# Folding the query norm's weights into the key norm's weights in a hybrid retention and sparse-attention layer

## The chip, the cores and the metric

The kernel runs on one core of one Trainium2 chip. The metric is the device time of one execution in microseconds, taken from runs of the whole program; a time of this kernel is the median of its runs. The engines are called as in the profile: PE (matrix products), PEld (its weight loads), DVE (vector), ACT (scalar, activations), POOL (GpSimd) and SP (the queue that issues the transfers).

## What is computed

One decoder layer on 1024 tokens with 16 meta tokens ahead of them. A normed stream is projected by one matrix; the columns feed a retention with 4 heads and a sparse attention with 8 heads of 64 columns, in which an indexer picks 256 keys for each query. Both results are projected, and a squared-ReLU MLP follows. What matters here is the norm of the attention's queries and keys:

```python
def rmsnorm(x, w):
    xf = x.astype(jnp.float32)
    y = xf * lax.rsqrt(jnp.mean(xf * xf, axis=-1, keepdims=True) + EPS)
    return y * w.astype(jnp.float32)

def sparse_attention(q, k, v, iq, ik, iw, q_gain, k_gain, rel_bias, pos, topk):
    qn = rmsnorm(q, q_gain) * (dh ** -0.5)       # q: (B,T,8,64)
    kn = rmsnorm(k, k_gain)                      # k: (B,T,64), one key for all heads
    ...
    logits = jnp.einsum('bchd,bckd->bchk', qb, k_sel)
```

Queries and keys meet only in that product over the 64 columns, and each of the two weight vectors has one entry for each column.

## The kernel before

The tokens are worked on in 8 blocks of 128. The code runs, in the order in which it is written, through these stages:

- The norm and the transposes of the input, block by block (`do_norm1`), the small projection (`small_proj`, the keys `kn` among it), the indexer's query projection (`index_q`, L246 to L248 into `psA`, copied to `nat`) and the indexer's scores (`index`): L356 and L357 on PE into `psB`, L359 on ACT into `rl`, L363 (L361 for the first head) on DVE, which adds up `sc`.
- The weights of the norms are loaded (`kgain` at L410, `qgain` at L412). The keys are normed (L432, DVE) and later transposed (L306).
- The query projection, L518 on: for each block the projection into `psA` (L246 to L248), a copy on ACT to `qn` (L528), its squares (L529, ACT), their sum (L531, DVE), the reciprocal root on POOL (L141, L142), the product with it (L533, DVE), the product with `qgain` (L534, POOL), and the store of the block to DRAM in `qd` (L535, SP). `qn` has the tag `rl` with two buffers, which it shares with `nat`; `psA` has three buffers, which index, query and retention projections share.
- The retention, for each of 4 heads: the weights are loaded (L210) and split into a high and a low half (L189 on ACT, L194 on POOL), then the meta tokens' part (`ret_meta`, L232 to L235) and 8 blocks (`ret_in`, L246 to L248 again, and `ret_out`). The split weights lie in 9 buffers of each half, which the weights of index, query and retention share, raw weights in 3.
- The search for the 256 keys by bisection (`topk`: L746 on DVE, L751 on ACT), the attention, the output projection and the MLP (L1002 to L1004, L1120 to L1122).

What stands on an engine's queue is not the order of the code. A planner that goes by a model of times puts every instruction into the queues and may move later work ahead; each queue then runs strictly in its order. So L432, which is written behind the indexer's last block, runs at 116 to 120 us, while the indexer's instructions go on to 197 us, and the bisection's L746, written near the end, runs from about 100 us on.

Of the kernel before, what the change touches and what calls it, by code (L numbers as in the profile page):

```python
# [14 lines left out]
ALU = mybir.AluOpType  # L15
# [66 lines left out]
def layer(ctx, tc, x, meta, norm1_w, w_in, ret_w, q_w, k_w, rel, w_out, norm2_w, w1, w2,  # L82
          ident_d, pack_d, hot_d, out, gam):
    nc = tc.nc
# [13 lines left out]
    def psA():  # L98
        return pp.tile([128, 512], F32, tag="A", name="psA", bufs=3)
# [18 lines left out]
    def bcast(src, n):  # L118
        return bass.AP(tensor=src.tensor, offset=src.offset, ap=[[0, 128], [1, n]])

    def shift(pool, n):

        nc.gpsimd.memset(pool.tile([128, n // 4], F32, name="shift", bufs=1), 0.0)
# [15 lines left out]
    def rsqrt(ms, k, f=1.0, P=128):  # L139
        y = small.tile([128, k], F32, name="rs_y", tag=f"rsy{k}", bufs=1 if k == 9 else 4)  # L140
        nc.gpsimd.tensor_tensor(y[:P], ms, epst[f][:P, :k] if isinstance(f, float) else f, op=ALU.add)  # L141
        nc.gpsimd.tensor_tensor(y[:P], y[:P], nhalf[:P, :k], op=ALU.pow)  # L142
        return y
# [97 lines left out]
    def proj(ps, b, hs, ls, c0, n):  # L241
        P = 128
        for d in range(8):
            uh, ul = u_sl(b, d)
            wh, wl = hs[d][:, c0:c0 + n], ls[d][:, c0:c0 + n]
            nc.tensor.matmul(ps[:P, :n], uh, wh, start=d == 0, stop=False)  # L246
            nc.tensor.matmul(ps[:P, :n], ul, wh, start=False, stop=False)  # L247
            nc.tensor.matmul(ps[:P, :n], uh, wl, start=False, stop=d == 7)  # L248
# [138 lines left out]
    for b in range(NB):  # L387
# [7 lines left out]
        if b:  # L395
# [13 lines left out]
    kgain = big.tile([128, 64], F32, name="kgain")  # L409
    nc.sync.dma_start(kgain, bcast(k_w, 64))  # L410
    qgain = big.tile([128, 64], F32, name="qgain")
    nc.sync.dma_start(qgain, bcast(q_w, 64))  # L412
    shift(const, 320)
    rgain = const.tile([128, 4], F32, name="rgain")
    nc.sync.dma_start(rgain, bass.AP(tensor=ret_w.tensor, offset=ret_w.offset, ap=[[1, 128], [128, 4]]))
# [12 lines left out]
                            op=ALU.add)  # L428
# [93 lines left out]
    for b in range(NB):  # L522
        ps = psA()
        proj(ps, b, hs, ls, 0, 512)
        p3 = ps.rearrange("p (h c) -> p h c", h=8)
        sq = big.tile([128, 8, 64], F32, tag="fg", name="sq", bufs=2)
        qn = wp.tile([128, 8, 64], F32, tag="rl", name="qn", bufs=2)
        nc.scalar.activation(qn, p3, AF.Copy)  # L528
        nc.scalar.activation(sq, qn, AF.Square)  # L529
        ssq = small.tile([128, 8], F32, name="ssq")  # L530
        nc.vector.tensor_reduce(ssq, sq, axis=mybir.AxisListType.X, op=ALU.add)  # L531
        r = rsqrt(ssq, 8, 64.0)
        nc.vector.tensor_tensor(qn, qn, r[:, :, None].to_broadcast([128, 8, 64]), op=ALU.mult)  # L533
        nc.gpsimd.tensor_tensor(qn, qn, qgain[:, None, :].to_broadcast([128, 8, 64]), op=ALU.mult)  # L534
        nc.sync.dma_start(qd[:, b], qn.rearrange("p a b -> p (a b)"))  # L535


# [655 lines left out]
def build(nc, inputs):  # L1193
    arrays, args = {}, []

    def add(name, a):
        arrays[name] = a
        args.append(nc.dram_tensor(name, a.shape, mybir.dt.from_np(a.dtype), kind="ExternalInput").ap())
    for name in _INS:
        a = np.ascontiguousarray(inputs[name])  # L1200
        if name in ("x", "w_in", "w_out", "w_ff1", "w_ff2"):
            a = a[0]
        add(f"in_{name}_dram", a)
    ident, pack, hot, gam = shape_constants()
    add("ident_dram", ident)
    add("pack_dram", pack)
    add("hot_dram", hot)
    args.append(nc.dram_tensor("out_0_dram", (T, D), F32, kind="ExternalOutput").ap())
    with tile.TileContext(nc, schedule_with_timeline_sim=True) as tc:
        layer(tc, *args, gam)  # L1210
    return arrays
# [10 lines left out]
```

## Time and profile before

| | |
|---|---|
| median of 3 runs | 1310.89 us (1308.47 to 1311.84) |
| the profiled execution's own time | 1311.07 us |
| its span | 1309.2 us |
| PE busy | 1248.5 us, 95% |
| DVE busy | 1037.7 us, 79% |
| ACT busy | 761.3 us, 58% |
| POOL busy | 236.2 us, 18% |
| granted TensorE clock, mean | 0.983 |

The span is the profiled part of an execution; 1.9 us of its own time lie around it. The granted clock is a share of the higher of TensorE's two levels (2.4 GHz): 1.00 in a stretch says that all of it ran at that level, 0.50 that all of it ran at 1.2 GHz. A busy share is an average over stages with different limits, so each stage is read by itself.

### The profile page before, as it was taken

Reading aid. Unit: us, or ns where it says so; the run is one execution under the profiler, and the core shown is the slowest. Engines: PE = TensorE matmul, PEld = TensorE weight load, DVE = VectorE, ACT = ScalarE, POOL = GpSimd, SP = SyncE. Lnnn points to the kernel's source line nnn. Section 1 sums busy time; section 2 is a strip of 40 time slices with the busy share of each in tenths; the row PEclk is TensorE's granted clock in tenths of the full one; section 3 lists DMA queues with packets and bytes.
Section 4 is the critical chain, followed back from the end, with each engine's and each line's share of the span. In section 5 each row is a group of like instructions: output and inputs, shape, how many; then the busy total and the mean of one; then the engine's idle time right before and its main releaser. Section 6 shows DMA issues by size and latency. Waiting matters only on the chain.

```text
span 1309.2 us, 18365 instructions
## 1 busy us (share of the span) xinstructions
PE 1248.5 (95%) x6032; PEld 1031.6 (79%) x6032; DVE 1037.7 (79%) x2297; ACT 761.3 (58%) x1612; POOL 236.2 (18%) x286
## 2 busy tenths in 40 slices
PE   5999989999999899999997999999999999999998
PEld 4888867777887677877786888888888888888887
DVE  5579999995459889976579887777788887887875
ACT  6567556787975777764356565555455444444442
POOL 4002373425244332200233000000000100000000
PEclk8999989999999899999998999999999999999999
DMA  8103031202021322212963444434539834344222
GB/s 277 61 18 91 17 97 63 74 9 73 9 73 39 131 98 83 84 60 89 324 225 119 169 145 153 145 145 144 186 129 345 327 112 181 137 153 173 94 95 97
DMA packets 101278, 165.05 MB, mean 126 GB/s; under 512 B 8712, under 2 KB 48944, under 8 KB 97472
## 3 DMA queue, kind: packets, MB, share of 16 engines
q1 hardware_dynamic: 101184, 163.90, 36.3%
q8 instruction: 47, 0.77, 0.2%
q14 instruction: 47, 0.39, 0.1%
HBM read 113.46 MB, written 51.85 MB: 126 GB/s over the span
## 4 chain that ended last, share of the span: by engine, by line
PE 69%; DVE 18%; ACT 5%; issue 3%; DMA 2%; POOL 1%; SPq 0%; ACTq 0%; DVEq 0%; POOLq 0%
PE psB L1121 5%; PE psB L1120 5%; PE psB L1122 5%; PE psB L1002 4%; PE psB L1003 4%; PE psB L1004 4%; PE psA L1003 4%; PE psA L1002 4%; PE psA L1004 4%; PE psA L246 3%; PE psA L247 3%; PE psA L248 3%; PE psA L1121 3%; PE psA L1120 3%; PE psA L1122 3%
## 5 line engine op out<-in xcount | busy, mean ns | idle before, releaser
L973 ACT ACTIVATE wh<-ga 128x512 fp32r<-128x512 f32 x144 | 87.5, 628 | 164.0 <-PE psB L1121 143.1
L246 PE MATMUL psA<-wh,uh 128*128 128x512 f32 x376 | 152.4, 406 | 2.9 <-DVE fg L487 2.2
L247 PE MATMUL psA<-wh,ul 128*128 128x512 f32 x376 | 150.1, 399 | 0.0
L248 PE MATMUL psA<-wl,uh 128*128 128x512 f32 x376 | 149.8, 399 | 0.0
L974 DVE TENSOR_TENSOR wl<-ga,wh 128x512 fp32r<-128x512 f32 x144 | 96.7, 688 | 49.4 <-ACT wh L973 48.8
L973 ACT ACTIVATE wh<-sum 128x512 fp32r<-128x512 f32 x128 | 78.8, 625 | 71.6 <-DVE sum L970 61.0
L751 ACT ACTIVATE jk_top<-sc,tcand 128x784 bf16<-128x784 f32 (+2 forms) x93 | 98.3, 1057 | 24.4 <-DVE tcand L821 20.3
L1121 PE MATMUL psB<-wh,wl 128*128 128x512 f32 x280 | 108.9, 389 | 0.0
L1122 PE MATMUL psB<-wl,wh 128*128 128x512 f32 x280 | 108.9, 389 | 0.0
L1120 PE MATMUL psB<-wh 128*128 128x512 f32 x280 | 106.8, 389 | 0.0
L974 DVE TENSOR_TENSOR wl<-sum,wh 128x512 fp32r<-128x512 f32 x128 | 88.6, 693 | 4.7 <-ACT wh L973 4.7
L246 PEld LDWEIGHTS psA<-wh,uh 128*128 128x128 f32 x376 | 71.9, 191 | 16.9 <-DVE fg L487 1.9
L248 PEld LDWEIGHTS psA<-wl,uh 128*128 128x128 f32 x376 | 71.7, 191 | 14.0
L247 PEld LDWEIGHTS psA<-wh,ul 128*128 128x128 f32 x376 | 71.8, 191 | 12.5
L1040 POOL COPY ga<-wl 128x1 f32<-128x1 f32 x8 | 6.6, 827 | 400.3 <-PE psB L1003 276.3
L746 DVE TENSOR_SCALAR_CACHE_REDUCE jk_cnt<-sc,tcand 128x400 bf16<-128x400 f32 (+2 forms) x93 | 70.3, 756 | 1.0
L359 ACT ACTIVATE rl<-psB,absw 128x320 f32<-128x320 f32 (+5 forms) x104 | 53.1, 556 | 31.0 <-DVE sc L363 16.8
L1121 PE MATMUL psA<-wh,wl 128*128 128x512 f32 x168 | 65.4, 389 | 0.0
L1122 PE MATMUL psA<-wl,wh 128*128 128x512 f32 x168 | 65.4, 389 | 0.0
L1120 PE MATMUL psA<-wh 128*128 128x512 f32 x168 | 64.9, 389 | 0.0
L194 POOL TENSOR_TENSOR wl<-wr,wh 128x512 fp32r<-128x512 f32 x44 | 61.3, 1419 | 19.0 <-ACT wh L189 15.6
L363 DVE SCALAR_TENSOR_TENSOR sc<-rl,sgnw,sc 128x320 f32<-128x320 f32 (+5 forms) x91 | 56.1, 651 | 8.2 <-ACT rl L359 7.2
(391 smaller groups left out, 3582.0 us busy)
## 6 DMA issues: line engine op xcount, KB each, us to landing
ga<-hid SPq DMA_DIRECT2D x28, 1024.0 KB, 5.2
wr<-in_w_ff_dram SPq DMA_DIRECT2D x34, 512.0 KB, 4.9
hid<-hs SPq DMA_DIRECT2D x48, 256.0 KB, 2.0
wr<-in_w_in_dram SPq DMA_DIRECT2D x32, 256.0 KB, 3.1
ysd<-ys SPq DMA_DIRECT2D x32, 256.0 KB, 2.4
ys<-ysd SPq DMA_DIRECT2D x32, 256.0 KB, 5.0
gb<-in_w_ff_dram SPq DMA_DIRECT2D x8, 1024.0 KB, 5.3
ga<-in_w_ff_dram SPq DMA_DIRECT2D x8, 1024.0 KB, 5.0
```

The costliest lines, as they stand in the source:

```text
L246: nc.tensor.matmul(ps[:P, :n], uh, wh, start=d == 0, stop=False)
L247: nc.tensor.matmul(ps[:P, :n], ul, wh, start=False, stop=False)
L248: nc.tensor.matmul(ps[:P, :n], uh, wl, start=False, stop=d == 7)
L751: nc.scalar.activation(jk_top[:, :ncol[i]], sc[i], AF.Sign, scale=-1.0, bias=cand[:, j:j + 1], accum_out=cnt[:, j:j + 1])
L973: nc.scalar.activation(view(hi), s, AF.Copy)
L974: nc.vector.tensor_tensor(view(lo), s, view(hi).bitcast(F32), op=SUB)
L1002: nc.tensor.matmul(ps, hi[:, a], uh[:, d], start=d == 0, stop=False)
L1003: nc.tensor.matmul(ps, lo[:, a], uh[:, d], start=False, stop=False)
L1004: nc.tensor.matmul(ps, hi[:, a], ul[:, d], start=False, stop=d == 3)
L1120: nc.tensor.matmul(ps[tb], ah[:, t], bh, start=j == 0 and m not in CONT, stop=False, skip_group_check=True)
L1121: nc.tensor.matmul(ps[tb], al[:, t], bh, start=False, stop=False, skip_group_check=True)
L1122: nc.tensor.matmul(ps[tb], ah[:, t], bl, start=False, stop=j == NO - 1, skip_group_check=True)
```

## The change

The two weight vectors are multiplied once, in place, right behind their loads, on DVE: `kgain` holds the product from then on, and the keys are normed with it. The multiplication of each query block with `qgain` on POOL is left out, and the store of the block follows the product on DVE.

```diff
     nc.sync.dma_start(kgain, bcast(k_w, 64))
     qgain = big.tile([128, 64], F32, name="qgain")
     nc.sync.dma_start(qgain, bcast(q_w, 64))
+    nc.vector.tensor_tensor(kgain, kgain, qgain, op=ALU.mult)
     shift(const, 320)
...
         nc.vector.tensor_tensor(qn, qn, r[:, :, None].to_broadcast([128, 8, 64]), op=ALU.mult)
-        nc.gpsimd.tensor_tensor(qn, qn, qgain[:, None, :].to_broadcast([128, 8, 64]), op=ALU.mult)
         nc.sync.dma_start(qd[:, b], qn.rearrange("p a b -> p (a b)"))
```

## Rows read from the trace of the kernel before

**Rows 1.** The page: span, busy time by engine, shares of the chain that ended last.

```profile
span 1309.2 us, 18365 instructions
PE 1248.5 (95%) x6032; PEld 1031.6 (79%) x6032; DVE 1037.7 (79%) x2297; ACT 761.3 (58%) x1612; POOL 236.2 (18%) x286
...
PE 69%; DVE 18%; ACT 5%; issue 3%; DMA 2%; POOL 1%; SPq 0%; ACTq 0%; DVEq 0%; POOLq 0%
```

**Rows 2.** Busy time by stretch: PE, PEld, DVE, ACT, POOL; granted clock; DMA share, GB/s.

```profile
140.00:174.00 34.00, 33.50 (x160) 28.43 (x159) 33.76 (x78) 20.94 (x41) 15.42 (x15) 1.00 0.08 32
174.00:190.00 16.00, 12.21 (x42) 8.33 (x41) 15.95 (x21) 8.00 (x17) 13.63 (x11) 0.68 0.54 153
...
720.00:1309.00 589.00, 585.29 (x2583) 484.30 (x2581) 468.27 (x749) 280.91 (x498) 8.26 (x18) 1.00 0.45 163
```

**Rows 3.** Timeline of PE: start, us, instruction [idle before it <- its releaser].

```profile
177.28 0.29 PE L232 MATMUL psA<-wl,um 128*16 128x256 f32 x1 [0.97 <-POOL wl L194]
...
185.59 0.63 PE L246 MATMUL psA<-wh,uh 128*128 128x512 f32 x1
```

**Rows 4.** Waits of PE, 60 to 206 us: in total, times, longest.

```profile
PE psA L246 <- ACT qn L528: 0.5, 1, 0.5
```

**Rows 5.** Timeline of POOL, 174 to 188 us.

```profile
174.25 2.97 POOL L194 TENSOR_TENSOR wl<-wr,wh 128x512 fp32r<-128x512 f32 x2
177.19 1.60 POOL L534 TENSOR_TENSOR qn<-qn,qgain 128x512 f32<-128x512 f32 x1
178.74 3.00 POOL L194 TENSOR_TENSOR wl<-wr,wh 128x512 fp32r<-128x512 f32 x2
181.71 1.59 POOL L534 TENSOR_TENSOR qn<-qn,qgain 128x512 f32<-128x512 f32 x1
183.27 4.23 POOL L194 TENSOR_TENSOR wl<-wr,wh 128x512 fp32r<-128x512 f32 x3
```

**Rows 6.** Timeline of DVE around the same stretch.

```profile
172.11 0.68 DVE L533 TENSOR_TENSOR qn<-qn,rs_y 128x512 f32<-128x512 f32 x1
172.71 1.00 DVE L363 SCALAR_TENSOR_TENSOR sc<-rl,sgnw,sc 128x320 f32<-128x320 f32 x2
...
174.32 1.78 DVE L533 TENSOR_TENSOR qn<-qn,rs_y 128x512 f32<-128x512 f32 x1
...
176.70 2.43 DVE L363 SCALAR_TENSOR_TENSOR sc<-rl,sgnw,sc 128x400 f32<-128x400 f32 x2
...
183.58 1.23 DVE L824 TENSOR_SCALAR tt<-tcnt 128x3 int32<-128x3 f32 x1
...
194.40 0.15 DVE L824 TENSOR_SCALAR tt<-tcnt 128x3 int32<-128x3 f32 x1
```

**Rows 7.** Timeline of ACT: two of the eight copies into `qn`.

```profile
166.25 0.60 ACT L528 ACTIVATE qn<-psA 128x512 f32<-128x512 f32 x1 [3.52 <-DMA qd<-qn]
...
184.17 0.59 ACT L528 ACTIVATE qn<-psA 128x512 f32<-128x512 f32 x1
```

**Rows 8.** Timeline of SP: the fifth store of a query block.

```profile
178.81 0.34 SPq L535 DMA_DIRECT2D qd<-qn  x1
```

**Rows 9.** Tile `qn`: duration ns min/median/max, first and last start us, forms.

```profile
L533 DVE TENSOR_TENSOR qn<-qn,rs_y x8: 680/686/1782, 137.9 to 199.3; 128x512 f32<-128x512 f32 x8
L534 POOL TENSOR_TENSOR qn<-qn,qgain x8: 1286/1295/1743, 138.8 to 200.4; 128x512 f32<-128x512 f32 x8
...
DMA to landing us min/median/max: 2.0/2.0/3.4
```

**Rows 10.** Tiles `kgain` and `qgain`, as rows 9.

```profile
L432 DVE SCALAR_TENSOR_TENSOR kn<-kn,rs_y,kgain x9: 269/273/1394, 116.0 to 120.3; 128x64 f32<-128x64 f32 x8, 16x64 f32<-16x64 f32 x1
...
L412 SPq DMA_DIRECT2D qgain<-in_q_norm_w_dram x1: 458/458/458, 11.7 to 11.7; - x1
...
DMA to landing us min/median/max: 3.2/3.2/3.2
```

**Rows 11.** Timeline of DVE in the start-up.

```profile
11.45 1.47 DVE L328 TENSOR_TENSOR wsl<-wrs,wsh 128x200 fp32r<-128x200 f32 x2
```

## The prediction, made before the changed kernel was run

> **What bounds the kernel now.** I read the page first [rows 1]. PE is busy 95% of the span and carries 69% of the chain that ended last, so in most of the kernel only what leaves PE without work, or lowers its clock, costs time. DVE carries another 18%, so the second question is where DVE takes PE's place. The busy times by stretch answer it [rows 2]. From 720 us on PE works 585.29 of 589.00 us: the MLP has nothing to give, and the change doesn't touch it. The lines that the change touches run from 138.8 to 202 us [rows 9]. From 140 to 174 us PE and DVE are both full (33.50 and 33.76 of 34.00 us). Then comes a hole: from 174 to 190 us PE works 12.21 of 16.00 us at a granted clock of 0.68, while DVE (15.95) is full and POOL (13.63) nearly so. The hole costs 16.00 - 12.21 = 3.8 us of idle PE and, as 0.68 of the clock means that 32% of the time's columns were not done, 0.32 x 16.00 = 5.1 us of lower clock: 8.9 us. Of TensorE's two levels 0.68 is 64% of the stretch at the lower one; the projection that starts at 185.59 us still takes 0.63 us for one matrix product there [rows 3]. The clock fell behind the idle pieces, at about 180 us.
>
> Who makes the hole? The waits of PE and the timelines of POOL, DVE, ACT and SP show two threads, and both run over POOL, whose queue has no gap from 174.25 to 187.50 us [rows 5].
> - Weights. The seven L194 there split the first retention head's weights. PE's L232 at 177.28 waited for one of them for 0.97 us [rows 3].
> - Buffers. The retention's first block projection, at 185.59, waited for a `psA` buffer until ACT's copy into `qn` of block 6, at 184.17 [rows 3, 4, 7]. Such a copy waits for the store of the block two before (block 4's own copy sat 3.52 us for one) [rows 7]. Block 4's product on DVE was done at 172.11 + 0.68 = 172.8 us [rows 6], but its L534 came up on POOL only at 177.19, behind other work, and its store left at 178.81 [rows 5, 8].
>
> A third effect is on DVE. While POOL works there, DVE's products stretch: a pair of L363 took 2.43 us against 1.00 for a somewhat smaller pair before, L533 1.78 against 0.68, a 128x3 `tt` 1.23 against 0.15 [rows 6].
>
> **The change part by part.** *Removed: eight L534 on POOL*, 1.3 us each, 1.6 in the hole [rows 5, 9]. Six of them lie outside the hole. There PE is full (140 to 174 us: 98.5%), so POOL's 6 x 1.3 us and what DVE gets back is covered by PE's own queue, and I cost it at nothing. If that cover were gone, each would return at most its own length to DVE, 6 x 1.3 = 7.8 us, and at least nothing, since DVE's counts and its reads of PSUM went on unstretched beside some of them.
>
> In the hole two go, 1.60 + 1.59 = 3.2 us of a POOL queue without gaps. The L194 behind them move up by as much, so the weights are ready up to 3.2 us sooner; and for 3.2 us DVE is not held. Both PE (through L194) and the last block of the indexer (through L363 on DVE) follow: -3.2 us. What is late next in that thread is the L194 themselves, some 10 us of which stay.
>
> *Moved: the stores.* The store's wait goes from POOL to DVE. Block 4's leaves SP's queue at about 172.8 and not at 178.81, 6.0 us sooner; block 5's at 174.32 + 1.78 = 176.1 and not behind the L534 that ends at 183.3, 7.2 us sooner [rows 5, 6, 8]. With 2.0 us to landing [rows 9], the buffer for block 6's copy is free at 174.8, and the copy at 184.17 could come up to 9 us earlier. SP has no other work between that is harmed: each store is still one issue, eight in all, and what is queued behind them (the next weights) moves up too. So the `psA` buffer stops being the retention's gate; the weights are. It can start with its first quarter of weights at about 177 us and then go at the pace of POOL's remaining L194.
>
> *The clock.* The trace of before doesn't show what the clock does when the hole narrows. Nothing returns if PE still starves (0), all 5.1 us if it never falls. The stretch before, with the same scores and PE 98.5% busy, ran at 1.00 [rows 2]; but the index scores of the hole are still paced by DVE beside some 10 us of L194, so PE will still have pauses. I take a third, 1.8 us.
>
> *Added: one product of 128x64 on DVE.* The nearest row is L432, of the same size and also on two tiles of SBUF: 0.27 us, up to 1.39 when held [rows 10]. It lies anywhere between the weights' landing and the keys' norm at 116 us; DVE has pauses there, so nothing. It adds a wait, though, for the load issued at 11.7 us that lands 3.2 us later, at 14.9 [rows 10]. Whatever the planner puts behind it on DVE waits too. The worst place is ahead of the L328 at 11.45 us [rows 11], where it would hold the splits of the first weights and the first blocks' norm for 14.9 - 11.45 = 3.5 us. Bounds 0 and +3.5; I take 0, since work that is written this late comes behind what is ready.
>
> Sum: -3.2 - 1.8 = -5.0 us against the profiled execution's 1311.07, so 1306.1; the median of the runs shown is 0.2 lower. I say 1306.0.
>
> *A rule beside it.* The rows show whole holds: the 128x3 operation's 1.23 us is about a POOL product's length [rows 5, 6]. The Trainium skill, SBUF — State Buffer, section "Who interferes with whom", says that a DVE instruction with two SBUF inputs, or in a two-port mode, and a GpSimd instruction that reads SBUF exclude each other for a whole instruction, and that issue order decides who is held. The trace agrees on the holds. By that rule all eight L534 together could return 8 x 1.3 = 10.4 us to DVE; but it also speaks against the change, since the L194 that move up take the same port in their place, and that is the second rival.
>
> **The rivals.**
> 1. The hole closes. With psA free early and weights coming, PE never idles long enough for the clock to fall: the whole 8.9 us return, 1302.2. For it: the copy moves by up to 9 us. Against it: L194 and DVE still pace the stretch.
> 2. No change. POOL's queue stays without gaps, only with other work: L194 hold DVE for as long as before, block 6's copy still stands in ACT's queue behind L359 that wait for DVE, and the planner, which has its own times for all this, leaves it where it is. What POOL saves is then given back as idle POOL later: 1310 to 1312. For it: DVE is full from 140 to 190 us whatever POOL does [rows 2].
> 3. Slower: the filler is used up. In the stretch from 140 to 174 us PE is full because query projections fill in between the indexer's scores. Faster `qn` buffers let the planner draw these projections forward. Then they end well ahead of 174 us, while the retention's weights cannot come sooner, as the split buffers are held by the query's weights until their last product. The hole opens earlier and is twice as long: +8.9 us, less the 3.2 that POOL gives back, 1316.8. It decides once the last query projection ends more than about 8 us before the first L194 of the retention. Against it: `psA` and the copies were not what filled PE there; DVE's and PE's totals were.
>
> **How the numbers follow.** Forecast (hole narrows, 1303 to 1309): 0.45. Rival 1 (1298 to 1303): 0.15. Rival 2 (1309 to 1313): 0.20. Rival 3 (1313 to 1319): 0.20. The range leaves out the lowest and the highest ends: 1298 to 1316. It holds the +3.5 us of the added wait on top of the forecast (1309.5) and on rival 2 (1314.6). About 0.3% (3.9 us) is what a measurement can tell from no change: faster means below 1307.0, slower above 1314.8. Faster: all of rival 1 and some 0.7 of the forecast, 0.15 + 0.33 = 0.48. Slower: most of rival 3, 0.16. The same: the rest, 0.36.
>
> **What would show it.** No POOL product with `qgain`; POOL's total down by about 11 us. Stores right behind L533. The copies into `qn` of blocks 6 and 7 well before 184 and 192 us. The hole about 174 to 190 us with PE over 13.5 of 16 us and a clock over 0.8; the indexer's last `sc` some 3 to 5 us earlier than 197 us; the MLP's 589 us as before, only shifted. It is wrong if the order of the queues has changed so far that PE idles elsewhere (any stretch from 200 to 720 us with a clock below 0.9 that was at 1.00), if query projections end before 165 us with a longer hole behind, or if DVE in the start-up stands still until about 15 us.

## The result, and the profile after

The changed kernel takes 1296.51 us (median of six runs, 1293.68 to 1299.81) where the kernel before takes 1312.13 in the runs beside it (1308.47 to 1314.08): a ratio of 0.9889, interval 0.9871 to 0.9906. It is 15.6 us faster; forecast were 5, and the range ended at 1298. The profiled execution of after took 1296.34 us, 14.7 less than that of before. In the profile, lines 413 to 533 of before are one higher in after (L533 is now L534), the others keep their numbers.

The page of after, its first lines and the chain that ended last:

```profile
span 1294.6 us, 18365 instructions
...
PE 1240.1 (96%) x6032; PEld 1025.8 (79%) x6032; DVE 1022.2 (79%) x2298; ACT 757.9 (59%) x1612; POOL 221.1 (17%) x278
...
PE 69%; DVE 19%; ACT 5%; issue 4%; DMA 2%; POOL 1%; SPq 0%; DVEq 0%; ACTq 0%
```

Against [rows 1] the span is 14.6 us shorter: PE is busy for 8.4 us less and idle for 6.2 us less (1309.2 - 1248.5 = 60.7, now 1294.6 - 1240.1 = 54.5). Its instructions are the same 6032; the shorter busy time is the granted clock, 0.983 on the mean before and 0.989 now: (1 - 0.983) x 1309.2 = 22.3 us lost before, (1 - 0.989) x 1294.6 = 14.2 after, 8.0 less. So more than half of the gain shows as clock, behind pauses that are gone.

Where? The busy times by stretch of after (PE, PEld, DVE, ACT, POOL; clock; DMA share, GB/s):

```profile
140.00:174.00 34.00, 34.00 (x165) 28.96 (x164) 33.72 (x80) 23.07 (x44) 14.30 (x14) 1.00 0.12 41
174.00:190.00 16.00, 12.52 (x56) 8.76 (x55) 16.00 (x26) 8.64 (x18) 12.07 (x10) 0.89 0.57 162
...
207.00:320.00 113.00, 109.70 (x567) 91.63 (x566) 90.99 (x324) 98.08 (x233) 43.62 (x65) 1.00 0.17 45
```

and the same view of before for a stretch that the prediction had not looked at:

```profile
207.00:320.00 113.00, 105.48 (x529) 87.10 (x528) 98.41 (x324) 90.88 (x216) 42.36 (x62) 0.97 0.17 45
```

From 140 to 190 us the picture is near the one forecast [rows 2]: PE's 33.50 became 34.00 and the hole's clock rose from 0.68 to 0.89, but PE works 12.52 us in it where the forecast asked for over 13.5. It still idles for 3.5 us, nearly all of it ahead of the indexer's L356, which waits for ACT's L359 (3.4 us in four waits). The surprise is the stretch from 207 to 320 us, the retention: 105.48 at 0.97 before, 109.70 at 1.00 now, 4.2 us less of idle PE and 3.4 us of clock, in a stage whose code the edit does not touch.

A table of lags shows it over the whole span. All matrix products of PE were sorted by their ends, and the columns that they stream were summed; for a point in the time of before, the entry is how much earlier (negative) the other kernel had streamed as many columns. (Another order brings other products first, and the pauses of two kernels lie at different points of the work, so a single entry may be off: after's -8.1 at 190 us is before's hole gone by, with after's own still to come. Lasting steps are real.)

```
us in the time of before    170    190    220    250    320    410    500    740
after                      -1.3   -8.1   -3.9   -9.5  -12.7  -14.3  -13.8  -14.4
old_order_small            -0.6   -4.7   -4.1   -7.0   -8.6   -7.1   -7.3   -5.8
new_order_load             +1.1   -1.4   +1.8   -2.4   -5.6   -7.1   -5.8   -7.3
```

About 4 us are there at 200 to 220 us; 9 more arise between 220 and 320 us, 1.6 up to 410. From there on little changes: from the first L1002 to the end of the last L1122 it takes 1305.3 - 681.6 = 623.7 us before and 1290.9 - 667.0 = 623.9 after. The other two rows are experiments, told below. One thing is to be kept from them here: `old_order_small`, which has before's order and only lacks the load, also gains 4.5 us between 220 and 320 us, and its clock from 207 to 320 us is 1.00 as well. So the surprise in the retention is not the order's alone.

The direct effects are as described. POOL's timeline of after has no product of the queries, and no gap while six L194 run:

```profile
174.03 8.76 POOL L194 TENSOR_TENSOR wl<-wr,wh 128x512 fp32r<-128x512 f32 x6
184.42 0.20 POOL L141 TENSOR_TENSOR rs_y<-ssq,eps 128x8 f32<-128x8 f32 x1 [1.64 <-DVE ssq L532]
184.58 1.29 POOL L194 TENSOR_TENSOR wl<-wr,wh 128x512 fp32r<-128x512 f32 x1
```

Six L194 are through at 174.03 + 8.76 = 182.8 us, where before the last three began at 183.27 [rows 5]. DVE is held by them as before: its timeline of after has

```profile
175.67 1.76 DVE L534 TENSOR_TENSOR qn<-qn,rs_y 128x512 f32<-128x512 f32 x1
...
178.16 2.26 DVE L363 SCALAR_TENSOR_TENSOR sc<-rl,sgnw,sc 128x320 f32<-128x320 f32 x2
180.34 1.24 DVE L824 TENSOR_SCALAR tt<-tcnt 128x3 int32<-128x3 f32 x1
```

which are the 1.78, 2.43 and 1.23 of [rows 6]. The tiles `qn` and `kgain` of after (duration ns min/median/max, first and last start):

```profile
L529 ACT ACTIVATE qn<-psA x8: 579/598/601, 129.9 to 177.7; 128x512 f32<-128x512 f32 x8
...
L413 DVE TENSOR_TENSOR kgain<-kgain,qgain x1: 215/215/215, 15.4 to 15.4; 128x64 f32<-128x64 f32 x1
```

The last copy into `qn` starts at 177.7 (192.2 before), that of block 6 at 167.55 (184.17 before [rows 7]). The retention's first product, at 185.59 before [rows 3], starts at 174.12 in after:

```profile
174.12 0.40 PE L246 MATMUL psA<-wh,uh 128*128 128x512 f32 x1
```

The added product costs 0.2 us at 15.4 us, right behind the load.

### The profile page after: what moved, and what is told of

Same layout as the page of the kernel before. It is cut to its first block, busy times and chain, and to the rows that moved or that the text cites. A ratio compares the mean times of both kernels' runs of the same rounds, so it can differ in the third digit from the quotient of the medians.

```text
span 1294.6 us, 18365 instructions
## 1 busy us (share of the span) xinstructions
PE 1240.1 (96%) x6032; PEld 1025.8 (79%) x6032; DVE 1022.2 (79%) x2298; ACT 757.9 (59%) x1612; POOL 221.1 (17%) x278
## 4 chain that ended last, share of the span: by engine, by line
PE 69%; DVE 19%; ACT 5%; issue 4%; DMA 2%; POOL 1%; SPq 0%; DVEq 0%; ACTq 0%
PE psB L1120 5%; PE psB L1121 5%; PE psB L1122 5%; PE psB L1002 4%; PE psB L1003 4%; PE psB L1004 4%; PE psA L1003 4%; PE psA L1002 4%; PE psA L1004 4%; DVE jk_cnt L746 3%; PE psA L246 3%; PE psA L247 3%; PE psA L248 3%; PE psA L1120 3%; PE psA L1121 3%
## 5 line engine op out<-in xcount | busy, mean ns | idle before, releaser
L1122 PE MATMUL psB<-wl,wh 128*128 128x512 f32 x280 | 108.9, 389 | 0.0
L751 ACT ACTIVATE jk_top<-sc,tcand 128x784 bf16<-128x784 f32 (+2 forms) x93 | 98.3, 1057 | 14.9 <-DVE tcand L821 12.5
L746 DVE TENSOR_SCALAR_CACHE_REDUCE jk_cnt<-sc,tcand 128x400 bf16<-128x400 f32 (+2 forms) x93 | 70.4, 757 | 1.0
L359 ACT ACTIVATE rl<-psB,absw 128x320 f32<-128x320 f32 (+5 forms) x104 | 52.9, 555 | 28.0 <-DVE sc L363 13.9
L1122 PE MATMUL psA<-wl,wh 128*128 128x512 f32 x168 | 65.4, 389 | 0.0
L194 POOL TENSOR_TENSOR wl<-wr,wh 128x512 fp32r<-128x512 f32 x44 | 60.3, 1390 | 19.2 <-ACT wh L189 13.9
L633 ACT ACTIVATE ph<-psB 128x512 fp32r<-128x512 f32 x72 | 41.4, 594 | 34.9 <-PE psB L628 26.8
```

What stands on the lines that cost most here:

```text
L746: nc.vector.tensor_scalar(jk_[:, :ncol[i]], sc[i], cand[:, j:j + 1], 0.0, op0=ALU.is_ge, op1=ALU.add, accum_out=cnt[:, j:j + 1])
L1122: nc.tensor.matmul(ps[tb], ah[:, t], bl, start=False, stop=j == NO - 1, skip_group_check=True)
```

## The experiments

Two things changed at once. POOL lost eight products (the load), and the planner, which sees shorter queues, put the instructions into another order: from about 138 us on the queues of after differ from those of before in hundreds of places on PE, DVE and ACT. "Order" below always means this. Where an experiment keeps an order, the queues of PE, DVE, ACT and SP were the same, instruction by instruction. Theory A is the forecast's: the load is what counts, the order only shifts. Theory B: the order is the larger part.

### Load and order apart

`old_order_small`: the kernel before, its order fixed with full products, which then run on 8 of their 512 columns (the rest of each block keeps its norm without the weight). What is left of each product takes 0.2 to 0.65 us on POOL, and the store still waits for it.

```diff
-nc.gpsimd.tensor_tensor(qn, qn, qgain[:, None, :].to_broadcast([128, 8, 64]), op=ALU.mult)
+RESIZED.append(nc.gpsimd.tensor_tensor(qn, qn, qgain[:, None, :].to_broadcast([128, 8, 64]), op=ALU.mult))
...
+    resize(nc, lambda p: replace(p, ap=[p.ap[0], (1, 8)]))   # once the order is fixed
```

> The queues of the kernel before, instruction for instruction (planned with the full product), but each of the eight products with qgain on POOL is cut to 128x8 elements after planning; the other columns thus go without the query's weights. Theory of the load (POOL's 1.3 us each, the DVE instructions held meanwhile and the late stores cost the time): most of the 15 us come back without any new order, 1296 to 1301. Theory of the order (the time is in the other order that the planner makes when the product is gone): the hole at 174 us shrinks by the 3.2 us of POOL, the stretch from 207 to 320 us stays, 1306 to 1310. The prediction's own sum would be 1306.

Measured: 1305.34 us beside 1311.38 of before; ratio 0.9954 (0.9936 to 0.9971). That is close to the forecast's own 1306, and a little below the range of the theory of the order.

`new_order_load`: the changed kernel in its own order, with a POOL addition of 128x512 into an unused tile put behind each block's L142.

```diff
+    if i.name in names:                          # names: L142 of the eight query blocks
+        out.append(replace(like, ins=[gain, gain], outs=[scratch]))
```

> The queues of the changed kernel, instruction for instruction, with eight products of 128x512 put back on POOL after planning, each right behind the root of its query block (L142), into a tile that nobody reads, and one fill of that tile at the start. POOL's load and its holds on DVE are those of before, in the new order; the store doesn't wait for POOL. Theory of the load: the gain is lost, 1306 to 1312. Theory of the order: 1297 to 1301, at most the 3 to 5 us of the hole come back.

Measured: 1303.59; ratio 0.9933 (0.9918 to 0.9948). Between the two theories again. The additions took 1.04 us each, the products of before 1.3 [rows 9], so a fifth of the load is missing.

`remove_alone`: the changed kernel without the added product on DVE (the keys are normed with their own weight alone, the queries with none).

```diff
-    nc.vector.tensor_tensor(kgain, kgain, qgain, op=ALU.mult)
```

> The changed kernel without the one product of both weights on DVE (the query's weights are left out); all other instructions stand in the same order. If the added product is hidden, as predicted: the time of the changed kernel within 1 us, 1295 to 1298. If its wait for the load costs in the start-up: up to 3.5 us less.

Measured: 1295.9; ratio 0.987 (0.9851 to 0.9889), the time of after. The added product costs nothing that these runs can tell.

The four corners:

```
                  with the load   small or no load
order of before        1311.4         1305.3
order of after         1303.6         1296.5
```

The load is worth 6.0 us in the one order and 7.1 in the other, the order 7.8 and 8.8. They add up, and neither theory holds alone: each makes about half of the gain. Which is the larger these runs do not settle, since the additions are shorter than the products and `old_order_small` keeps a remnant of them. In the table of lags `old_order_small` is at -4.7 at 190 us and -7.0 at 250 us and ends at -5.8 (what it gains up to 320 us and loses again behind is not explained); `new_order_load` is at -2.4 at 250 us and gains until 410.

### How far orders scatter

If the order is worth 8 us, is that a property of this change, or luck? Four kernels ran the same small load in other orders.

`planned_256_small`: as `old_order_small`, but its order was fixed with half a product (four of eight heads), and with the added product.

```diff
+nc.gpsimd.tensor_tensor(qn[:, :4], qn[:, :4], qgain[:, None, :].to_broadcast([128, 4, 64]), op=ALU.mult)
```

> The changed kernel (weights folded), with a POOL product of 128x256 behind L534's place when it is planned, cut to 128x8 on the chip (a few columns of one head get the query's weights twice). The load on the chip is that of the changed kernel, the order a third one, that differs from both in hundreds of places. Theory of the load: 1296 to 1300, whatever the order. Theory of the order: the time is that of this order alone; halfway if the planner's longer chain sets it (1300 to 1306), anywhere from 1293 to 1312 if orders scatter.

Measured: 1311.68; ratio 0.9997 (0.9985 to 1.0009).

`planned_small`: a product of 128x8 in the plan and on the chip.

```diff
+nc.gpsimd.tensor_tensor(qn[:, 0, :8], qn[:, 0, :8], qgain[:, :8], op=ALU.mult)
```

> The changed kernel with a POOL product of 128x8 ahead of each store, in the plan and on the chip (eight columns of one head get the query's weights twice). POOL's load is the changed kernel's plus 8 x 0.2 us, the order a fourth one. If a longer planned chain makes a worse order step by step (0: 1296.5, 256 columns: 1311.7, 512 columns: 1305.3 with the same small load don't say so): near 1297. If orders scatter: anywhere from 1293 to 1312, most likely 1300 to 1306.

Measured: 1306.03; ratio 0.9965 (0.995 to 0.998).

`planned_128_small`: planned with two heads (128 columns), run on 8.

```diff
+nc.gpsimd.tensor_tensor(qn[:, :2], qn[:, :2], qgain[:, None, :].to_broadcast([128, 2, 64]), op=ALU.mult)
```

> As planned_256_small, with a product of 128x128 when it is planned, cut to 128x8 on the chip. Its order stands nearer to that of the changed kernel (294 lines of PE's queue differ, against 547 from before). If nearness in the queue says what it costs: 1296 to 1300. If orders scatter: anywhere from 1293 to 1312.

Measured: 1306.43; ratio 0.9966 (0.9951 to 0.9981).

`planned_384_small`: planned with six heads.

```diff
+nc.gpsimd.tensor_tensor(qn[:, :6], qn[:, :6], qgain[:, None, :].to_broadcast([128, 6, 64]), op=ALU.mult)
```

> As planned_256_small, with a product of 128x384 when it is planned, cut to 128x8 on the chip. Its order stands nearer to that of before (304 lines of PE's queue differ, 565 from the changed kernel's). If nearness says what it costs: 1304 to 1307, as before's order with the small product (1305.3). If orders scatter: anywhere from 1293 to 1312.

Measured: 1309.63; ratio 0.9985 (0.9973 to 0.9998).

Planned with 0, 8, 128, 256, 384 and 512 columns, but run with next to none, the kernel takes 1296.5, 1306.0, 1306.4, 1311.7, 1309.6 and 1305.3 us. There is no trend in the size. Six orders of nearly the same work scatter over 15 us, and that of the changed kernel is the best of them by 9.

One difference besides the order is left: in the other five a short product on POOL still stands between DVE's product and the store, in after nothing does. Its direct effect does not explain the 9 us. By lag against after the five are level or ahead at 190 us (by 0.2 to 3.2 us), the last store of a query block is issued by 200 us, and at 320 us the five are 4.9 to 7.4 us behind. Kernels without that product scatter too, as further edits below show, each of which changes a little work (1304.2 to 1308.6 us).

### Where in the retention an order costs

The waits of PE between 207 and 320 us of before (in total us, times, longest):

```profile
PE psB L506 <- DVE sm L503: 2.7, 2, 1.5
PE psB L505 <- ACT jk L511: 2.4, 1, 2.4
PE psB L499 <- ACT qkT L497: 1.6, 1, 1.6
```

of `old_order_small` from 205 to 320 us:

```profile
PE psB L505 <- ACT jk L511: 2.4, 1, 2.4
PE psB L499 <- ACT qkT L497: 1.6, 1, 1.6
PE psB L506 <- DVE sm L503: 1.5, 1, 1.5
```

of `new_order_load`, same stretch:

```profile
PE psA L246 <- DVE fg L488: 1.8, 1, 1.8
PE psA L232 <- POOL wl L194: 1.4, 3, 0.8
PE psB L500 <- ACT qkT L498: 1.2, 1, 1.2
```

and of after, from 193 to 310 us:

```profile
PE psA L232 <- POOL wl L194: 1.4, 3, 0.8
PE psB L500 <- ACT qkT L498: 1.1, 1, 1.1
PE psA L246 <- DVE fg L488: 0.7, 1, 0.7
```

These longest waits go with the order, not with the load. (The clock does not: from 207 to 230 us, with the same 2.4 us wait, it was 0.93 in before and 1.00 in `old_order_small`.) The longest of before's order, 2.4 us for `jk`, is read from ACT's timeline of before:

```profile
218.89 0.95 ACT L751 ACTIVATE jk_top<-sc,tcand 128x784 bf16<-128x784 f32 x1 [1.78 <-DVE tcand L821]
...
219.96 1.06 ACT L751 ACTIVATE jk_top<-sc,tcand 128x912 bf16<-128x912 f32 x1
...
221.14 1.16 ACT L751 ACTIVATE jk_top<-sc,tcand 128x1040 bf16<-128x1040 f32 x1
...
222.30 0.26 ACT L511 ACTIVATE jk<-psB 128x128 bf16<-128x128 f32 x1
```

Three counts of the bisection, 3.2 us, stand in a row on ACT ahead of a square of 0.26 us (L511) that PE needs before it can write the next block into the same PSUM bank (L505). In after the same kinds are interleaved one by one:

```profile
217.73 0.95 ACT L751 ACTIVATE jk_top<-sc,tcand 128x784 bf16<-128x784 f32 x1 [0.48 <-DVE tcand L827]
...
218.68 0.26 ACT L512 ACTIVATE jk<-psB 128x128 bf16<-128x128 f32 x1
...
219.34 1.06 ACT L751 ACTIVATE jk_top<-sc,tcand 128x912 bf16<-128x912 f32 x1
...
220.38 0.38 ACT L498 ACTIVATE qkT<-psB 128x256 f32<-128x256 f32 x1
220.64 1.17 ACT L751 ACTIVATE jk_top<-sc,tcand 128x1040 bf16<-128x1040 f32 x1
```

Are these counts what makes the order matter? Four kernels cut the counts to 8 columns in either order (small load), on ACT or on DVE; the thresholds that the counts are held against were made constants, so that all rounds still run.

```diff
+    cut_counts(nc)        # L751 (or L746): [128, n] -> [128, 8], once the order is fixed
```

`old_act_cut`, `new_act_cut` (L751 on ACT, 1.06 us on the mean, became 0.3):

> old_order_small (the queues of before, the eight POOL products cut) with the 93 counts of the bisection on ACT (L751, 1.05 to 1.26 us each) cut to 8 columns after planning, so that the bisection finds wrong thresholds; no queue changes. Together with new_act_cut it asks where the 8.8 us between the two orders (1305.3 and 1296.5 with the same small load) arise. If they arise because ACT's counts stand ahead of the retention's own ACT instructions (PE's L505 waits for ACT's L511, L499 for L497): the two orders come within 3 us of each other. If they don't: 7 us or more stay between them. This kernel itself: 1285 to 1300.

> The changed kernel with the 93 counts of the bisection on ACT (L751) cut to 8 columns after planning; no queue changes, the thresholds are wrong. Counts on ACT as the place of the order's price: within 3 us of old_act_cut. Otherwise 7 us or more below it. By itself: 1282 to 1295.

Measured: 1304.39 (0.994, 0.9917 to 0.9963) and 1296.25 (0.988, 0.9861 to 0.9899): 8.1 apart, as without the cut (8.8), so by the end times, the expectation's own measure, ACT's counts are not the place. Both times lie above the ranges expected of them.

`old_dve_cut`, `new_dve_cut` (102 counts of L746 on DVE, 0.78 us on the mean, became 0.21):

> old_order_small with the bisection's counts on DVE (L746, 0.62 to 1.3 us each) cut to 8 columns after planning; no queue changes, the thresholds are wrong. Together with new_dve_cut: if the 8.8 us between the orders arise because DVE's counts stand ahead of the retention's DVE instructions (PE's L506 waits for L503, L246 for L487), or because DVE is full: the orders come within 3 us of each other. Otherwise 7 us or more stay. By itself: 1270 to 1295, since DVE is full from 100 to 207 us.

> The changed kernel with the bisection's counts on DVE (L746) cut to 8 columns after planning; no queue changes, the thresholds are wrong. Counts on DVE as the place of the order's price: within 3 us of old_dve_cut. Otherwise 7 us or more below it. By itself: 1265 to 1290.

Measured: 1295.01 (0.9867, 0.9849 to 0.9886) and 1291.36 (0.9844, 0.9825 to 0.9863): 3.7 apart instead of 8.8, between the two answers that were set down.

By lag the difference is made in two stages. New order against old:

```
us in the time of the old-order kernel   190    230    250    320    350    400    500    740
uncut                                   +0.2   -3.0   -2.4   -4.6   -5.3   -7.4   -6.7   -8.6
L751 on ACT cut                         +0.1   -2.1   +0.3   -2.1   -2.0   -3.2   -2.2   -6.8
L746 on DVE cut                         +1.3   +1.0   +2.1   +0.5   +0.2   -1.9   -2.7   -1.9
```

Up to 350 us, 5.3 us of the order's worth shrink to 2.0 without ACT's counts and vanish without DVE's. So up to 350 us the orders differ little without the counts. How the counts do it is shown for one wait only, the 2.4 us for `jk`: the cut on DVE also takes 102 x 0.57 = 58 us of work off an engine that was busy for 98 of the 113 us from 207 to 320 us, so counts that stand ahead of short instructions and a full DVE are not told apart. The other 3 us or so arise behind 350 us; the cuts move them about, and I have no row for them. They stay open.

### Other edits, other orders

`squares_last`: the four squares of a group move behind its fourth block, so that no product of PE waits for one.

```diff
-        nc.scalar.activation(jk, po, AF.Square, scale=2.0 * 128.0 ** -0.5, accum_out=ssr[:, q:q + 1])
         if q == 3:
+            for j in range(4):
+                nc.scalar.activation(jk, p2[:, 128 * j:128 * j + 128], AF.Square, ..., accum_out=ssr[:, j:j + 1])
```

> The changed kernel with the four squares of a group of four retention blocks (L512) moved from the end of each block to behind the fourth, in one go; the work is the same. PE writes the next block's part of the same PSUM bank and waits for the square of the block before; moved, this wait is gone. Theory A, the retention stage is paced by how the orders of ACT and DVE place its short instructions: freeing one hand-over lets the planner place them better, 1288 to 1294 us, and the gain stands between 207 and 350 us. Theory B, any edit makes another order and orders scatter by some 15 us about 1306: then it lands anywhere from 1296 to 1312 us, above the changed kernel more likely than below, and the lag moves on its own from 350 us on too.

Measured: 1304.28; ratio 0.9955 (0.994 to 0.9971): 7.8 above after. Its lag against after steps from 1.8 to 8.4 us between 290 and 300 us, where the next head's weights come in. PE, clock and the rest for that stretch, in after and then in `squares_last`:

```profile
290.00:305.00 15.00, 13.58 (x75) 11.03 (x74) 7.53 (x25) 14.02 (x32) 13.81 (x14) 1.00 0.56 146
```

```profile
290.00:305.00 15.00, 9.24 (x46) 7.70 (x46) 11.90 (x23) 11.74 (x32) 13.54 (x14) 0.79 0.46 119
```

with these waits of PE from 285 to 305 us in `squares_last`:

```profile
PE psB L500 <- ACT qkT L498: 3.2, 1, 3.2
PE psB L507 <- DVE sm L504: 2.6, 1, 2.6
```

The wait for the square is gone, and others of the same kind are there: `sm` stood behind 3.8 us of mask work (L767, L768) on DVE, `qkT` behind a count and four short instructions on ACT. Its theory A falls.

`square_from_psum`: ACT squares the query from PSUM rather than from its copy.

```diff
-        nc.scalar.activation(sq, qn, AF.Square)
+        nc.scalar.activation(sq, p3, AF.Square)
```

> The changed kernel where ACT squares the query's projection from PSUM instead of from its copy, so that the square need not wait for the copy; a query's norm is shorter by one hand-over, the work is the same. The path of the norm is not what ends last in the trace of the changed kernel (the stretch from 140 to 174 us is full on PE), so by its own effect the time should stay: 1294 to 1298 us if the order of the queues matters little for this edit. If orders scatter whatever the edit, as the six orders at the same load did, it lies above, 1300 to 1310 us, with the loss arising behind 205 us, in stages that the edit does not touch.

Measured: 1307.18; ratio 0.9972 (0.9962 to 0.9983). At 190 to 230 us its lag against after is 1.9 us, at 250 us 4.0, at 320 us 9.6: as expected of scatter, the loss comes where the edit is not.

`split_shared_h0`: every second low half of the first retention head's weights on DVE instead of POOL.

```diff
-st["w", h] = load_cols(w_in, [(o + 128 * h, 128) for o in (RQ, RK, RV, RG)])
+st["w", h] = load_cols(w_in, [(o + 128 * h, 128) for o in (RQ, RK, RV, RG)], alt=h == 0)
```

> The changed kernel with every second low half of the first retention head's weights made on DVE (L194, 0.68 us each) and not on POOL (1.3 to 1.5 us, during which DVE's products are held). If holds cost DVE more than the work itself: the hole at 174 to 190 us gets 2 to 4 us shorter; with the order as it is 1292 to 1295. But this is planned anew, and if orders scatter by 15 us the result may be anywhere from 1291 to 1310; then only the hole tells (PE over 13.5 of 16 us).

Measured: 1308.58; ratio 0.9975 (0.9961 to 0.9989). Two microseconds ahead of after at 200 to 230 us, 11 behind at 320. The hole gave the sign that was asked for: PE works 14.06 of its 16 us, at a clock of 1.00.

`split_shared_all`: the same for all heads (`alt=True`).

> The changed kernel with every second low half of the retention's weights, of all heads, computed on DVE instead of POOL (split_shared_h0 did so for head 0 alone, and gained 2 us at 200 to 230 us before it lost 13 elsewhere). The hole from 174 to 190 us is paced by POOL's products; sharing them should close about 2 us more of it. Theory A, what split_shared_h0 lost was its order, and has nothing to do with shared splits: then this one lands anywhere among the orders, 1292 to 1312 us, but again shows a gain of about 2 us at 200 us. Theory B, DVE's added time is what cost: DVE gets about 20 more products of 0.5 us between 180 and 350 us where it is nearly full, so 1306 to 1314 us, with a lag that grows evenly over that stretch.

Measured: 1304.15; ratio 0.9943 (0.9921 to 0.9964). It is 4.9 us ahead of after at 190 to 230 us, more than twice what I had expected, since the hole is all but closed:

```profile
174.00:190.00 16.00, 15.02 (x74) 11.61 (x73) 15.97 (x31) 9.03 (x19) 9.28 (x9) 1.00 0.54 155
```

Then it gives back 3.6 us between 230 and 250 us, and 6 more between 380 and 400, and ends 5.8 behind at 740 us. The lag grows in steps, which speaks for the order; but DVE also carries 98.52 us from 207 to 320 us where it carried 90.99 in after, so the added work is not excluded. What it does show is the price of the rest of the hole, about 4.9 us at its place.

### What of the load costs

`new_order_fill`: as `new_order_load`, with fills in place of the additions. A fill occupies POOL and reads nothing.

```diff
+        out.append(replace(fill, outs=[scratch]))     # 128x1024 bf16
```

> The changed kernel with its own order on every queue, plus eight fills of an unused 128x1024 tile on POOL, one behind each block's L142, where new_order_load had eight products. A fill reads nothing. It asks what of the product's load costs time. Theory A, the holds: a POOL product holds DVE for its whole length, and DVE paces the stretch from 140 to 250 us; fills hold nothing, so the time stays that of the changed kernel, 1296 to 1298 us. Theory B, POOL's own time: the products lengthen POOL's gapless queue from 174 to 190 us and so delay the weights behind it, whoever is held; then fills of about 1 us give what the products gave, 1302 to 1304 us, and fills of about half of that 1299 to 1300 us. The fill's duration is read from the trace; the lag at the same work of PE at 190 and at 250 us tells A from B where the whole time is close.

Measured: 1299.59; ratio 0.9912 (0.9888 to 0.9936), between the two theories. The fills took as long as the additions to within 0.1 us:

```profile
L125 POOL MEMSET scratch<- x9: 947/952/953, 0.7 to 189.9; 128x1024 bf16 x9
```

but against after the lag at 250 us is 2.2 us with fills and 7.1 with additions. Of these, 0.6 and 0.7 us are there at 140 us, before they can be the load's. What remains at 250 us is 1.6 us for POOL's own time against 6.4, a quarter; by the end times (3.1 and 7.1 us above after) it is some two fifths. The rest needs the reads. What the reads do is seen where DVE's L534 meets the one or the other. In `new_order_fill` POOL, then DVE:

```profile
162.72 0.95 POOL L125 MEMSET scratch<- 128x1024 bf16 x1
```

```profile
163.36 0.69 DVE L534 TENSOR_TENSOR qn<-qn,rs_y 128x512 f32<-128x512 f32 x1
```

and in `new_order_load`:

```profile
167.97 1.04 POOL L141 TENSOR_TENSOR scratch<-eps 128x512 f32<-128x512 f32 x1
```

```profile
168.04 1.51 DVE L534 TENSOR_TENSOR qn<-qn,rs_y 128x512 f32<-128x512 f32 x1 [0.80 <-POOL rs_y L142]
```

Beside the fill it takes its usual 0.69 us; beside the addition 1.51, from 168.04 to 169.55, 0.5 us past the addition's end at 169.01. The Trainium skill, SBUF — State Buffer, section "Who interferes with whom", says so: a DVE instruction with two SBUF inputs contends with a GpSimd instruction that reads SBUF, not with one that only writes it. Both runs agree.

## Why the prediction was wrong

**The step that failed** is the sum's silence on everything behind the hole. It reads -3.2 - 1.8 and ends at 190 us: what lies behind has no term, so it was put at nothing, and no row was given for that. For the MLP this held (623.7 and 623.9 us); for the stages between it did not. The order there is the planner's answer to the shorter queues, and it was worth 7.8 to 8.8 us of the 15.6. In the text the order stood only as a danger (the third rival, and the last sentence on what would be wrong). So the best case among the rivals was the closed hole, 1302.2, and the range ended 4 us below it, while orders of nearly the same work scatter by 15 us. That it came out as a gain is luck: of the six orders the one that came is the best, and the middle of the six, about 1306, is where the forecast stood.

**The hole** came out near its size, by parts that did not. In before's order (`old_order_small`) the load returned 6.0 us against 5.0 forecast, and the hole itself

```profile
174.00:190.00 16.00, 13.66 (x66) 10.34 (x64) 16.00 (x26) 9.01 (x18) 12.44 (x11) 0.89 0.57 164
```

loses 2.3 us of idle PE and 0.11 x 16 = 1.8 of clock, 4.1 in place of 8.9: -4.8. The clock's third was too little (3.4 of 5.1 us came back), the idle part too much (3.8 to 2.3, 1.5 us, not 3.2). And the threads were weighed wrongly. The prediction looked for the hole in the weights and the buffers and named the stretched DVE third; but of PE's waits in before from 60 to 206 us, those for ACT's `rl`, which waits for DVE's L363, were the largest:

```profile
PE psB L356 <- ACT rl L359: 2.8, 4, 0.8
PE psA L232 <- POOL wl L194: 1.0, 1, 1.0
```

The fills say the same: POOL's own time is a quarter to two fifths of what the additions cost, the reads that hold DVE the rest.

**The six products outside the hole**, costed at nothing: near enough in before's order (0.6 us at 170 us), not in the new one, where the additions had cost 1.8 us by 170 us (2.6 of lag against after, less 0.8 that is there from 30 us on) and PE 0.84 us of the stretch from 140 to 174 us:

```profile
140.00:174.00 34.00, 33.16 (x153) 26.79 (x153) 32.88 (x74) 20.31 (x38) 14.37 (x15) 1.00 0.11 40
```

**The stores and the buffer**: the outcome right, the reason not. The copies come up to 16.6 us earlier (block 6), PE's wait for `qn` [rows 4] is not among those of after, and the retention starts at 174.12. But block 6's copy had not waited for its buffer at 184.17: block 4's store left at 178.81 and took 2.0 us to land [rows 8, 9], and the copy stood behind ACT's L359, as the second rival said. In `old_order_small` the store leaves 2.9 us sooner, and the copy still comes behind two L359 at 180.34, the retention's first product at 181.76. It is the new order that moved the copy. **The added product**: right, 0 (`remove_alone`). **POOL's total**: 15.1 us less, where I said about 11. **The last `sc`** of the indexer came 1.8 us sooner (195.5 for 197.2), not 3 to 5.

**The rivals.** The hole did not close (1): `split_shared_all` all but does it. No change (2) is excluded by `old_order_small`. The filler (3): in after PE is full up to 174 us, the last query projection ends at 173.4 (174.65 before), and the hole did not widen; but its mechanism, an order that moves a gap elsewhere, is real, and its price is part of that of the order, here with the other sign.

## What to carry to other kernels

Where a planner fills the queues, an edit has two prices: what its instructions cost, which the trace shows, and another order of everything behind them, which it doesn't; keep the order and shrink the instruction, or keep the instruction's load in the new order, to tell them apart. Before a gain is put down to an idea, run the same work in a few other orders: here they scatter by 15 us (1.2%), more than the 6 to 7 us that the load itself was worth. And cost a POOL instruction that reads SBUF by the DVE instructions that it holds, not only by its place in POOL's queue.

## What was unexpected of the hardware

- POOL's time and its reads can be told apart: eight fills of 0.95 us made the kernel 3.1 us longer, eight additions of 1.04 us 7.1.
- A pause can cost twice: the 290 to 305 us stretch of `squares_last`, where two waits sum to 5.8 us, ran at a granted clock of 0.79, another 0.21 x 15 = 3.2 us, where after ran at 1.00. It need not: from 174 to 190 us `squares_last` works 11.97 of 16 us at a clock of 1.00, before 12.21 at 0.68.
- With DVE's counts cut the changed kernel still took 1291.4 us, 5.1 less than uncut, though DVE gave up 58 us of work.
